# A hybrid decoder step on one core: TensorE leaves mixers' pieces longer in nine projection tiles, the planner's transfer model changes, and the norms' spread product gets 128 rows

## The chip, the core and the metric

The kernel runs on one core of a Trainium2 chip. The metric is the device time of one execution in microseconds; 1324.06 to 1327.06 us were measured for the kernel before, median 1326.87. The engines named here are TensorE (PE in the rows, its weight loader PEld), VectorE (DVE), ScalarE (ACT), GpSimd (POOL) and SyncE (SP), whose queue issues all transfers.

## What is computed

One layer of a hybrid decoder, for a prompt of 1024 rows and 8 sample groups of 8 rows (T = 1088 rows together, width 1024), all in float32:

```python
h = _rmsnorm(x, g_mix_in)
gate_a, x_a, q, k, v, z_c, xbc, dt_raw = _split_cols(h @ w_in)
x_a, lru_buf_new = _causal_conv(x_a, lru_buf, conv_a_w, conv_a_b)
h_a, lru_h_new = _rg_lru(x_a, lru_h0, ...)
out_a = h_a * jax.nn.gelu(gate_a)                          # mixer A
out_b = _combine_branches([... for (w, d) in DILATED])     # mixer B: 6 heads, three dilations
xbc = jax.nn.silu(_causal_conv(xbc, ssd_buf, conv_c_w, conv_c_b)[0])
y_c, ssd_h_new = _ssd(xs, dt, A, Bm, Cm, ssd_h0, chunk)    # mixer C: chunked scan
out_c = _rmsnorm((y_c + d_skip * xs) * jax.nn.silu(z_c), ssm_norm)
x = x + _rmsnorm(concat(out_a, out_b, out_c) @ w_out, g_mix_out)
g_f, u_f = jnp.split(_rmsnorm(x, g_ffn_in) @ w_gate_up, 2, axis=-1)
x = x + _rmsnorm((jax.nn.silu(g_f) * u_f) @ w_down, g_ffn_out)
```

The updated states and the new rows of the key and value caches are outputs too.

## The kernel before

**Layout and products.** Activations lie transposed, 128 features on the partitions and the T rows along them, cut into three groups of 364, 362 and 362 columns (`GROUPS`). Each float32 operand of a large product is split into two rounded parts (float32r), and `mm3` makes one product of three: high with high, high with low, low with high. `x3` makes these three for one block of 128 of the contraction; eight such steps fill a bank for one projection tile and one group.

**Stages.** `w_in` has 23 tiles of 128 outputs. Tiles 0 and 1 are made in `first_products` while the input's norm is taken, tiles 2 to 22 in `projections`, in the order: 2 to 8 the convolved inputs of mixer C, 9 to 11 value, query and key of the first pair of heads, 12 to 14 z, 15 to 17 the second pair of heads, 18 to 20 the third, 21 and 22 the gate. A finished bank goes through `spill` to SBUF or to DRAM (`pd`). Beside this main task run the mixers: `lru`, `convs` and `time_steps`, then `scan` with a `chunk` for each 128 rows, then `attention` (a pair p of heads starts when tile V_T[p] + 2, that is tile 11, 17 or 20, is emitted), `norm_c` and `gate`; their outputs go to `mixd` in DRAM and come back as operands of `w_out`. Then follow `first_out` (first group), `second_half` (waits for `mixers_done`), `gate_up` and `down`.

**The planner.** All instructions are ordered while the program is built. `Flow` keeps a time `now` for TensorE and models of the other engines' queues; `note` takes an operation of VectorE, ScalarE, GpSimd or SP, and `step` emits the one that is ready and has the best rank at the moment when its engine would be idle. A transfer costs QUEUE on SP, then FLIGHT, then its bytes by RATE, one transfer after the other, and its data count as there RECEIPT later. TensorE's own work is in tasks (generators), each of which yields a condition; `run` goes through the tasks in order and advances the first one whose condition holds, mixers ahead of main, so that main's steps fill what the mixers leave. Most of the mixers' conditions ask `ok(...)`: have the operands' writers ended by `now`, with SIGNAL + MARGIN (0.35 us) to spare? The planner's times decide only the order; on the chip every instruction waits for its semaphores, each engine in the order planned.

**The norms.** `inverse_norm` turns a row of sums of squares (128 x w, w about 363) into 1/rms, spread over 128 partitions: three products of one column sum over the partitions, VectorE and GpSimd take the power and split it into two parts, `tr` transposes 128 x 6 values to 6 rows, VectorE spreads these over w columns (6 rows, each non-zero in its own third), and one product with a stationary operand of ones, 6 rows by 128 columns, puts the value of each column on all 128 partitions. The buffer for the 6 rows is the one item of the lane `spread`, 128 x 364 in float32r, of which only rows 0 to 5 are ever written. `inverse_norm` is called by `first_scale` (three times), `norm_c` (three), `out_norm` (twice for each of three groups) and `finish` (two).

Of the kernel before, what the change touches and what calls it, by code (L numbers as in the profile page):

```python
# [35 lines left out]
XA_T, XBC_T, Z_T, GATE_T = 0, 2, 12, 21  # L36
V_T = (9, 15, 18)
W_OUT_T, W_GU_T, W_DN_T = 23, 31, 75
QT = T // 4

PLAIN = 4
PRODUCTS = (1, 6, 2, 7, 5, 4, 3)

# [51 lines left out]
class Rot:  # L95
    def __init__(self, items):
        self.items, self.i = items, -1
# [35 lines left out]
class Flow:  # L133
# [4 lines left out]

    RANKS = {"prep": 0, "norm": 1, "mix": 2, "main": 3}

    SIGNAL, MARGIN = 0.15, 0.2
    QUEUE, FLIGHT, RECEIPT, RATE = 0.475, 0.65, 0.95, 360e3

    def __init__(self):
        self.now, self.tasks = 0.0, []
        self.rank, self.count = 0, 0
        self.idle = {e: 0.0 for e in ("vector", "scalar", "gpsimd", "sync")}
        self.ready = {e: [] for e in self.idle}
        self.dma, self.table = 0.0, None
        self.open = []  # L150
        self.locks = [0.0, 0.0]
        self.place, self.top = {}, 0
        self.wr, self.rd = np.zeros(1 << 18), np.zeros(1 << 18)
# [56 lines left out]
    def ok(self, *aps, write=False):  # L210
        uses = self.uses(aps, write)
        self.advance(self.now)
        return self.done(uses) + self.SIGNAL + self.MARGIN <= self.now and not self.pending(uses)

    def free(self, x):

# [97 lines left out]
    def run(self):  # L314
        idle = 0
        while self.tasks:
            for task in self.tasks:
                if task.cond is None or task.cond():
                    with self.prio(task.cls):
                        try:  # L320
                            task.cond = next(task.gen)
                        except StopIteration:
                            self.tasks.remove(task)
                    idle = 0
                    break
            else:
                self.now += 0.05
                idle += 1
                assert idle < 20000
        self.advance(1e9)  # L330
# [34 lines left out]
class Trunk:  # L365
# [150 lines left out]
    def projections(self):  # L516

        F = self.flow
        for i in range(2, W_OUT_T):
            parts = self.use(i)  # L520
            for g, (c0, w) in enumerate(GROUPS):
                yield lambda: self.lmain.ok() and F.ok(*parts)
                bank = self.lmain.take()
                for k in range(KT):
                    self.x3(bank[:, :w], parts, k, slice(c0, c0 + w), k == 0, k == KT - 1)
                    if k == KT - 1:
                        yield lambda: self.scaled > g
                        if g == 0 and XBC_T < i < XBC_T + 7:
                            yield lambda: self.conv_raws is not None and self.conv_raws.ok()
                            self.padded[i] = self.conv_raws.take()  # L530
                            self.pad(self.padded[i], self.I["ssd_conv"][i - XBC_T])
                        if i >= GATE_T:
                            yield lambda: self.c_done
                        self.spill(i, g, bank[:, :w])
                        self.lmain.give(bank)
                        self.free_at[g] = i + 1
                        if g == 2:
                            self.emitted = i + 1
                    yield None
            if i == DT_AFTER:  # L540
                yield from self.project_dt()
# [28 lines left out]
    def inverse_norm(self, ssum, n, lane, spread):  # L570

        nc, F = self.nc, self.flow
        w = ssum.shape[-1]
        yield lambda: F.ok(ssum) and lane.ok() and self.rstd.ok()
        bank = lane.take()
        at = [min(c, w - 128) for c in range(0, w, 128)]
        b = len(at)
        for c, o in enumerate(at):  # L580
            self.mm(bank[:, c:c + 1], ssum[:, o:o + 128], self.k(K_ONE, 1), start=True, stop=True)
        held = self.rstd.take()
        r, both = held[:, 0:b], held[:, 4:4 + 2 * b].rearrange("p (c q) -> p c q", q=2)
        hi, lo = both[:, :, 0], both[:, :, 1]
        with self.prio("prep"):
            nc.vector.tensor_scalar(r, bank[:, :b], 1.0 / n, EPS, op0=ALU.mult, op1=ALU.add)
            nc.gpsimd.tensor_tensor(r, r, self.half[:, :b], op=ALU.pow)
            nc.vector.tensor_copy(hi.bitcast(F32R), r)
            nc.vector.tensor_sub(lo, r, hi)
        yield lambda: F.ok(both) and spread.ok()  # L590
        rows = bank[0:2 * b, 128:256]
        self.tr(rows, held[:, 4:4 + 2 * b], self.k(K_ID))
        whole = spread.take()
        lent, spread, full = spread, whole[0:2 * b, :w], (b - 1) * 128
        with self.prio("prep"):
            nc.vector.tensor_mul(spread[:, :full].rearrange("p (c t) -> p c t", c=b - 1),
                                 rows[:, None, :].to_broadcast([2 * b, b - 1, 128]),
                                 bc(self.k(K_ROW, b - 1)[0:2 * b], 128))
            nc.vector.tensor_scalar(spread[:, full:], rows[:, 128 - (w - full):], self.k(K_ROW + b - 1, 1)[0:2 * b],
                                    None, op0=ALU.mult)  # L600
        self.rstd.give(held)
        yield lambda: F.ok(spread)
        self.mm(bank[:, :w], self.ones[0:2 * b], spread, start=True, stop=True)
        lent.give(whole)
        return bank

# [58 lines left out]
    def setup(self):  # L665
        nc, I = self.nc, self.I
        xr = [self.alloc(T) for _ in range(8)]
        squares = [self.alloc(364) for _ in range(6)]
        sq, ssum = Rot(squares), self.alloc(T)
        self.splits.append(self.pair())  # L670
        with self.prio("prep"):
            nc.vector.memset(self.half, -0.5)
            self.zeros = self.alloc(256)
            nc.vector.memset(self.zeros, 0.0)
            self.warm(2 * WARM)
            nc.scalar.activation(squares[1][:, 0:4], self.half, AF.Square)
            nc.sync.dma_start(self.cols, I["cols"])
            for k in range(KT):
                g = self.col(C_GMI + k)
                for c0, w in GROUPS if k < 4 else [(0, T)]:  # L680
                    sl = slice(c0, c0 + w)
                    nc.sync.dma_start(xr[k][:, sl], I["xT"][k][:, sl])
                    if k == 0 and c0 == 0:
                        self.first_weights(0, 256)
                    nc.scalar.activation(self.XH[:, k, sl], xr[k][:, sl], AF.Copy, scale=g)
                    nc.vector.scalar_tensor_tensor(self.XL[:, k, sl], xr[k][:, sl], g, self.XH[:, k, sl].bitcast(F32),
                                                   op0=ALU.mult, op1=ALU.subtract)
                if k == 1:
                    self.first_weights(256, 1024)
                if k == 4:  # L690
                    self.prep(2)
            nc.sync.dma_start(self.const, I["consts"][:, 0:K_TRI])
            nc.vector.tensor_copy(self.ones, self.k(K_ONE))
            for i in range(2):
                self.pad(self.padded[XA_T + i], I["lru_conv"][i])
            self.pad(self.padded[XBC_T], I["ssd_conv"][0])
            for c0, w in GROUPS:
                sl = slice(c0, c0 + w)
                for k in range(KT):
                    s, x = sq()[:, :w] if k else ssum[:, sl], xr[k][:, sl]  # L700
                    nc.scalar.activation(s, x, AF.Square)
                    if k:
                        nc.vector.tensor_add(ssum[:, sl], ssum[:, sl], s)
        return ssum
# [828 lines left out]
    def make_stream(self):  # L1533


        self.units = [(j, which, (0, 1)) for j in range(PLAIN // 2, NF // 2) for which in range(2)]
        self.units += [(j, which, (1,)) for j in range(PLAIN // 2) for which in range(2)]
        self.items = [lambda pair: self.plain(pair, LATE_T)]
        self.items += [lambda pair, t=W_OUT_T + n: self.plain(pair, t) for n in range(KT - 1)]
        self.plain_base = len(self.items)  # L1540
        for f in range(PLAIN):
            for which in range(2):
# [12 lines left out]
        order = [LATE_T] + [W_OUT_T + n for n in range(KT - 1)]  # L1555
        order += [W_GU_T + which * NF + f for f in range(PLAIN) for which in range(2)]
        self.tiles_of = dict(enumerate(order))
# [526 lines left out]
```

## Time and profile before

| what | value |
|---|---|
| median of three runs (lowest, highest) | 1326.87 us (1324.06, 1327.06) |
| the profiled execution's own time | 1324.27 us |
| its span, first to last instruction | 1322.5 us |
| TensorE busy | 1294.4 us (98%), 8883 matmuls |
| VectorE, ScalarE, GpSimd busy | 931.3 (70%), 557.1 (42%), 46.5 us (4%) |
| mean granted clock of TensorE | 0.996 |

In the rows, `PE bank L434` is a matmul of the helper `mm` (line 434) and `PE bank L438` a transpose; operations of the other engines all carry line 347, where the planner's wrapper records them, so a row is told apart by its tile names and shape. A shape such as `6*128 6x362` on TensorE is rows x columns of the array in use, then the operand that streams. Busy time of TensorE is modelled from pipelined records: full does not mean at its peak, and the loader's pauses say more.

### The profile page before, as it was taken

To read this page: it belongs to the slowest core of one execution; us is meant where nothing else is said; L and a number is where in the kernel's file an instruction comes from. 1 tells how busy PE (TensorE), PEld (TensorE's weight loads), DVE (VectorE), ACT (ScalarE), POOL (GpSimd) and SP (SyncE) were. 2 spreads that over 40 slices of the span, in tenths; PEclk is the share of its full clock that TensorE was granted. 3 is DMA by queue.
4 is the path that set the end of the run, shared out by engine and by line. 5 is a ranking of instruction groups with operands and counts; after the bars stand their busy time and mean duration, and the time that the engine had idled before them with its cause. 6 is when DMAs were issued, how large, how long until landed. Compare 5 with 4: busy or idle time off the path is not lost.

```text
span 1322.5 us, 22885 instructions
## 1 busy us (share of the span) xinstructions
PE 1294.4 (98%) x8883; PEld 1236.8 (94%) x8883; DVE 931.3 (70%) x1867; ACT 557.1 (42%) x1063; POOL 46.5 (4%) x60
## 2 busy tenths in 40 slices
PE   9999999999999999999999999999999999999997
PEld 8999888899899889989999999999999999999786
DVE  7799795764867977789756666666658856557852
ACT  7364461671675874445222222222223442433312
POOL 0000000000000002420000000000000000000000
PEclk9999999999999999999999999999999999999999
DMA  6122466536737446442132212221023566866651
GB/s 215 29 69 73 125 193 186 166 97 193 215 95 195 142 136 189 159 148 92 46 98 98 78 39 81 98 98 66 34 98 130 174 225 214 301 215 195 193 180 48
DMA packets 92922, 179.38 MB, mean 136 GB/s; under 512 B 15010, under 2 KB 60814, under 8 KB 92814
## 3 DMA queue, kind: packets, MB, share of 16 engines
q1 hardware_dynamic: 92814, 177.93, 43.0%
q8 instruction: 69, 1.13, 0.4%
q14 instruction: 39, 0.32, 0.1%
HBM read 138.61 MB, written 39.28 MB: 135 GB/s over the span
## 4 chain that ended last, share of the span: by engine, by line
PE 76%; DVE 9%; DMA 9%; ACT 2%; issue 2%; SPq 1%; DVEq 0%; POOLq 0%; POOL 0%; ACTq 0%
PE bank L434 74%; DVE t L347 9%; ACT t L347 2%; DMA t<-pd 2%; DMA t<-in_w_in_t 2%; PE bank L438 2%; DMA t<-mixd 2%; SPq L347 1%; DMA t<-yd 1%; DMA t<-eacd 1%; DMA t<-in_w_gu_t 0%; DMA t<-hidd 0%; DMA t<-in_w_out_t 0%; DMA mixd<-t 0%; DMA pd<-t 0%
## 5 line engine op out<-in xcount | busy, mean ns | idle before, releaser
L434 PE MATMUL bank<-t,t 128*128 128x272 f32 (+7 forms) x8505 | 1265.1, 311 | 15.7 <-DVE t L347 12.5
L434 PEld LDWEIGHTS bank<-t,t 128*128 128x128 f32 (+1 forms) x8505 | 1197.7, 186 | 64.5 <-DVE t L347 21.1
L347 DVE TENSOR_TENSOR t<-t,t 128x512 fp32r<-128x512 f32 (+13 forms) x599 | 440.1, 760 | 102.2 <-ACT t L347 93.5
L347 ACT CAST t<-t 128x512 fp32r<-128x512 f32 (+7 forms) x314 | 220.6, 724 | 437.1 <-PE bank L434 178.4
L347 DVE TENSOR_TENSOR t<-t,bank 128x272 f32<-128x272 f32 (+4 forms) x283 | 126.5, 454 | 123.0 <-PE bank L434 122.4
L347 DVE TENSOR_TENSOR t<-bank,t 128x512 fp32r<-128x512 f32 (+11 forms) x227 | 111.7, 511 | 77.1 <-ACT t L347 42.0
L347 ACT ACTIVATE t<-t,t 128x128 f32<-128x128 f32 (+17 forms) x212 | 132.6, 666 | 29.3 <-DVE t L347 13.9
L347 ACT ACTIVATE t<-t 128x272 f32<-128x272 f32 (+9 forms) x173 | 91.5, 537 | 112.7 <-DVE t L347 98.6
L347 POOL TENSOR_TENSOR t<-t,t 128x362 f32<-128x362 f32 (+3 forms) x41 | 43.6, 1077 | 1106.4 <-DVE t L347 1097.6
L347 DVE CAST t<-t 128x1024 fp32r<-128x1024 f32 (+6 forms) x91 | 45.1, 496 | 46.5 <-PE bank L434 34.5
L347 ACT COPY t<-bank 128x272 f32<-128x272 f32 (+7 forms) x122 | 44.5, 373 | 76.9 <-PE bank L434 63.9
L347 DVE TENSOR_TENSOR t<-t 128x272 f32<-128x272 f32 (+8 forms) x147 | 68.2, 465 | 5.3 <-ACT t L347 2.0
L347 DVE SCALAR_TENSOR_TENSOR t<-t,t,t 128x1112 f32<-128x1112 f32 (+6 forms) x68 | 56.9, 861 | 6.0 <-ACT t L347 5.2
L438 PE MATMUL bank<-t,t 128*128 128x128 f32 (+5 forms) x354 | 54.1, 274 | 4.8 <-DVE t L347 3.0
L438 PEld LDWEIGHTS bank<-t,t 128*128 128x128 f32 (+5 forms) x354 | 39.6, 138 | 13.4 <-DVE t L347 7.6
L347 ACT ACTIVATE t<-bank 128x272 f32<-128x272 f32 (+7 forms) x55 | 23.4, 429 | 61.4 <-PE bank L434 60.1
L347 DVE CUSTOM_DVE_ANT_0 t<-bank,t 128x512 f32<-128x512 f32 (+4 forms) x75 | 39.9, 548 | 5.5 <-PE bank L434 5.2
L347 ACT CAST t<-bank 128x512 fp32r<-128x512 f32 (+2 forms) x72 | 35.2, 514 | 19.3 <-PE bank L438 18.9
L347 DVE SCALAR_TENSOR_TENSOR t<-t,t,bank 128x362 f32<-128x362 f32 (+4 forms) x55 | 27.9, 549 | 4.0 <-PE bank L434 2.9
L347 DVE SCALAR_TENSOR_TENSOR t<-t,t 128x1024 f32<-128x1024 f32 (+4 forms) x26 | 20.3, 805 | 2.7 <-ACT t L347 1.5
L347 ACT ACTIVATE t<-bank,t 128x362 f32<-128x362 f32 (+1 forms) x29 | 15.5, 561 | 11.5 <-PE bank L434 11.5
L347 DVE SCALAR_TENSOR_TENSOR t<-t 128x54 f32<-128x54 f32 (+5 forms) x33 | 14.7, 447 | 3.9 <-DMA t<-yd 3.1
(20 smaller groups left out, 76.4 us busy)
## 6 DMA issues: line engine op xcount, KB each, us to landing
t<-in_w_dn SPq DMA_DIRECT2D x66, 512.0 KB, 3.7
t<-in_w_gu_t SPq DMA_DIRECT2D x52, 512.0 KB, 4.5
hidd<-t SPq DMA_DIRECT2D x44, 272.0 KB, 2.1
t<-in_w_in_t SPq DMA_DIRECT2D x21, 512.0 KB, 4.4
t<-hidd SPq DMA_DIRECT2D x44, 176.0 KB, 3.8
t<-in_w_out_t SPq DMA_DIRECT2D x15, 512.0 KB, 3.9
t<-pd SPq DMA_DIRECT2D x24, 256.0 KB, 4.4
t<-in_xT SPq DMA_DIRECT2D x24, 181.0 KB, 3.6
```

What stands on the lines that cost most here:

```text
L347: self.flow.note(self.name, what, args, kw, lambda: getattr(self.engine, what)(*args, **kw))
L434: self.flow.product(out, [w, x], start, d, lambda: self.nc.tensor.matmul(out, w, x, **how))
L438: self.flow.product(out, [x], True, d, lambda: self.nc.tensor.transpose(out, x, ident))
```

## The change

Three edits, which share no lines:

- In main's loop over tiles, a flag `patient` is set for tiles 9 to 17. While it is set, `ok` asked by a mixer's task wants 0.5 us more since the operands' last writer (0.85 instead of 0.35 us). Nothing else asks differently.
- The transfer model's RECEIPT goes from 0.95 to 1.25 us and its RATE from 360 to 280 KB per us (KB of 1000 bytes).
- The spread product takes all 128 partitions of the buffer and of the ones; at the start two VectorE copies fill the buffer with zeros.

```diff
@@ -38,6 +38,7 @@
 W_OUT_T, W_GU_T, W_DN_T = 23, 31, 75
 QT = T // 4
 
+PATIENT = 18
 PLAIN = 4
 PRODUCTS = (1, 6, 2, 7, 5, 4, 3)
 
@@ -138,11 +139,11 @@
 
     RANKS = {"prep": 0, "norm": 1, "mix": 2, "main": 3}
 
-    SIGNAL, MARGIN = 0.15, 0.2
-    QUEUE, FLIGHT, RECEIPT, RATE = 0.475, 0.65, 0.95, 360e3
+    SIGNAL, MARGIN, PATIENCE = 0.15, 0.2, 0.5
+    QUEUE, FLIGHT, RECEIPT, RATE = 0.475, 0.65, 1.25, 280e3
 
     def __init__(self):
-        self.now, self.tasks = 0.0, []
+        self.now, self.tasks, self.patient, self.patience = 0.0, [], False, 0.0
         self.rank, self.count = 0, 0
         self.idle = {e: 0.0 for e in ("vector", "scalar", "gpsimd", "sync")}
         self.ready = {e: [] for e in self.idle}
@@ -210,7 +211,7 @@
     def ok(self, *aps, write=False):
         uses = self.uses(aps, write)
         self.advance(self.now)
-        return self.done(uses) + self.SIGNAL + self.MARGIN <= self.now and not self.pending(uses)
+        return self.done(uses) + self.SIGNAL + self.MARGIN + self.patience <= self.now and not self.pending(uses)
 
     def free(self, x):
 
@@ -315,6 +316,7 @@
         idle = 0
         while self.tasks:
             for task in self.tasks:
+                self.patience = self.PATIENCE * (self.patient and task.cls == "mix")
                 if task.cond is None or task.cond():
                     with self.prio(task.cls):
                         try:
@@ -517,6 +519,7 @@
 
         F = self.flow
         for i in range(2, W_OUT_T):
+            F.patient = XBC_T + 7 <= i < PATIENT
             parts = self.use(i)
             for g, (c0, w) in enumerate(GROUPS):
                 yield lambda: self.lmain.ok() and F.ok(*parts)
@@ -600,7 +603,7 @@
                                     None, op0=ALU.mult)
         self.rstd.give(held)
         yield lambda: F.ok(spread)
-        self.mm(bank[:, :w], self.ones[0:2 * b], spread, start=True, stop=True)
+        self.mm(bank[:, :w], self.ones, whole[:, :w], start=True, stop=True)
         lent.give(whole)
         return bank
 
@@ -691,6 +694,8 @@
                     self.prep(2)
             nc.sync.dma_start(self.const, I["consts"][:, 0:K_TRI])
             nc.vector.tensor_copy(self.ones, self.k(K_ONE))
+            for o in (0, 364 - 256):
+                nc.vector.tensor_copy(self.spread.items[0][:, o:o + 256], self.zeros)
             for i in range(2):
                 self.pad(self.padded[XA_T + i], I["lru_conv"][i])
             self.pad(self.padded[XBC_T], I["ssd_conv"][0])
```

## Rows read from the trace of the kernel before

**Rows 1.** Windows by stage: busy us (instructions) of each engine, granted clock, DMA.

```profile
139.00:330.00 191.00, 185.71 (x1306) 167.84 (x1305) 132.74 (x334) 88.13 (x196) 3.15 (x6) 1.00 0.56 165
401.00:509.00 108.00, 100.72 (x655) 93.27 (x654) 88.29 (x222) 76.41 (x156) 0.00 (x0) 0.98 0.55 158
509.00:602.00 93.00, 90.64 (x591) 87.53 (x591) 74.47 (x132) 41.55 (x73) 34.89 (x30) 0.98 0.52 164
602.00:1210.00 608.00, 607.71 (x4535) 607.13 (x4535) 401.23 (x703) 192.80 (x349) 0.00 (x0) 1.00 0.38 124
```

**Rows 2.** Timeline of SP: issue of the spills and of mixer outputs.

```profile
142.54 0.33 SPq L347 DMA_DIRECT2D pd<-t  x1
...
300.09 1.50 SPq L347 DMA_DIRECT2D mixd<-t  x2
...
328.87 0.32 SPq L347 DMA_DIRECT2D pd<-t  x1
...
400.15 0.51 SPq L347 DMA_DIRECT2D pd<-t  x1
```

**Rows 3.** Groups by line, TensorE, 139 to 330: busy, mean, idle and releaser.

```profile
L434 PE MATMUL bank<-t,t 128*128 128x362 f32 (+11 forms) x1170 | 176.0, 319 | 5.1 <-DVE t L347 5.1
```

**Rows 4.** Weight loads by shape, whole span: busy us, mean ns, idle before.

```profile
L434 PEld LDWEIGHTS bank<-t,t 128*128 128x128 f32 x8025 | 1164.7, 189 | 47.0 <-DVE t L347 14.6 <-issue 8.0 <-ACT t L347 4.5
...
L434 PEld LDWEIGHTS bank<-t,t 6*128 6x128 f32 x14 | 2.5, 181 | 3.9 <-DVE t L347 1.9 <-issue 1.7
```

**Rows 5.** Timeline of the loader around one spread product.

```profile
541.45 0.18 PEld L434 LDWEIGHTS bank<-t,t 6*128 6x128 f32 x1 [0.23 <-issue]
541.80 0.46 PEld L434 LDWEIGHTS bank<-t,t 128*128 128x128 f32 x3 [0.17 <-issue]
```

**Rows 6.** Windows of TensorE with one spread product and without.

```profile
319.31:320.96 1.65, 1.65 (x10) 1.00 0.40 148
317.60:319.25 1.65, 1.65 (x12) 1.00 0.81 207
```

**Rows 7.** Timeline of TensorE, 139 to 509: start, length, count, pause before.

```profile
157.65 4.73 PE L434 MATMUL bank<-t,t 128*64 128x128 f32 x40 [1.33 <-DVE t L347]
...
239.13 4.04 PE L434 MATMUL bank<-t,t 128*128 128x128 f32 x23 [1.11 <-DVE t L347]
...
314.34 2.92 PE L434 MATMUL bank<-t,t 128*128 128x1 f32 x18 [0.95 <-DVE t L347]
...
333.26 1.09 PE L438 MATMUL bank<-t,t 128*128 128x128 f32 x8 [0.98 <-DMA t<-pd]
...
401.22 11.55 PE L434 MATMUL bank<-t,t 128*128 128x364 f32 x69
...
413.78 0.41 PE L434 MATMUL bank<-t,t 128*128 128x384 f32 x1 [1.01 <-ACT t L347]
...
414.95 9.83 PE L434 MATMUL bank<-t,t 128*128 128x384 f32 x49 [0.75 <-DVE t L347]
...
435.20 6.81 PE L434 MATMUL bank<-t,t 128*128 128x364 f32 x37 [1.02 <-ACT t L347]
...
508.92 6.43 PE L434 MATMUL bank<-t,t 128*128 128x1 f32 x30 [2.13 <-DVE t L347]
```

**Rows 8.** Timeline of VectorE at the start.

```profile
4.43 0.60 DVE L347 SCALAR_TENSOR_TENSOR t<-t,t,t 128x364 fp32r<-128x364 f32 x1 [3.27 <-ACT t L347]
```

**Rows 9.** DMA issues: count, KB of one, median us to landing.

```profile
t<-in_w_dn SPq DMA_DIRECT2D x66, 512.0 KB, 3.7
...
t<-in_w_in_t SPq DMA_DIRECT2D x21, 512.0 KB, 4.4
...
t<-pd SPq DMA_DIRECT2D x24, 256.0 KB, 4.4
```

**Rows 10.** The chain that ended last, in order of time, one piece.

```profile
404.10 7.16 DMA t<-pd
```

**Rows 11.** Window of TensorE: granted clock after the busy columns.

```profile
410.00:420.00 10.00, 8.24 (x39) 7.51 (x38) 7.97 (x19) 5.69 (x10) 0.00 (x0) 0.83 0.69 172
```

## Prediction, made before the changed kernel was run

> **What bounds the kernel now.** I read the stage windows first: TensorE is busy for 607.71 of the 608 us from 602 to 1210, so in the second half only shorter TensorE work can save time; before that it is busy for 185.71 of 191 us, 100.72 of 108 and 90.64 of 93 [rows 1]. The matmul stream is the bound and its pauses are what there is to win: 5.3, 7.3 and 2.4 us in the three stretches. Tiles 9 to 17 run from about 139 to 330 us: their first spill to DRAM is issued at 142.54, the last of tile 17 at 328.87, that of tile 20 at 400.15 [rows 2]. Then come TensorE's pauses with their releasers, VectorE first among them [rows 3]. Busy is modelled, though, so I also read the weight loader beside the matmuls, where a lost slot shows as a pause although the busy column is full, and last the times from DMA issue to landing.
>
> **The spread product with 128 rows.** There are 14 of them [rows 4]: three in the input's norm, three in mixer C's, six in the two norms behind w_out, two in the last. Around each the loader pauses twice, for nothing that the profile names: at 541.45 the six-row weights are loaded after a pause of 0.23 us, at 541.80 the next 128 rows after 0.17 [rows 5]; the same stands at each one that does not wait for VectorE, while between other products of the stream it does not pause. That is 0.40 us, 14 x 0.40 = 5.6 us. The other price: a stretch of 1.65 us with the product has 10 matmuls, the like stretch just before it 12 [rows 6]; a slot of this size is 11.55/69 = 0.167 us [rows 7], so two are 0.33 us and the 14 are 4.7 us. I take 5.1, ends 4.7 and 5.6, and zero if the rival below is right. All 14 stand among products that TensorE has queued behind them, so what they give back shortens the path. The product's columns stay the same, so its own streaming does not change. Added are two VectorE copies of 128x256; the nearest row is a larger operation, 0.60 us for 128x364, so at most 1.2 us together. They need only the zeros, and VectorE idles 3.27 us before 4.43 [rows 8]: that idle hides them. Were they put later, at their place in the code, VectorE would carry them in front of the sums of the first norm; by 1.2 us at the most that norm, and the bank it frees, would come later.
>
> On this part two pages differ. The Trainium skill ("TensorE: Matmul & The Clock Gate", section "Why this matters for your kernels") says that a single product with a contraction of 32 takes the same time as one of 128, which would make this part worth 0; and for the load alone the rows agree, 181 ns with six rows and 189 with 128 [rows 4]. The Trainium skill ("TensorEngine Tiling (Array Packing)", section "Key Properties") says that a change of tiling mode drains TensorE, which would make it worth what the two pauses show; the pauses are there [rows 5], and they agree with this one; the sum rests on the pauses alone.
>
> **Patience in tiles 9 to 17.** While main is in these tiles, a mixer's piece counts its operands as ready half a microsecond later in the planner's time, and the planner puts main's step (three products, 3 x 0.167 = 0.5 us) in front of it. On the chip the piece then meets its operands later by about one such step, and a pause of TensorE in front of it shrinks by up to 0.5. All pauses in this stretch that wait for VectorE add up to 5.1 us [rows 3]: 1.33, 1.11 and 0.95 are shown [rows 7], five smaller ones, none over 0.6, share the other 1.7. Taking 0.5 off the three long ones and 1.6 of the rest gives 3.1 us. Upper end 5.1, lower end 0: the pieces' shape stays, and so do the drains between shapes.
> What is late next? With the pieces move the VectorE and ScalarE operations that read their banks, and on SP their stores (yd, mixd) behind main's spills; nothing of main waits for those stores. GpSimd has only the norms' powers and a few memsets there. What the mixers lose is slack that they have: the next head pair needs tile 17's spill (328.87) and the last one tile 20's (400.15) [rows 2], so from there they wait for main, and main comes earlier by what is saved. From tile 18 on the patience is off, and mixers go first again.
>
> **The transfer model.** For 512 KB the planner expected 0.475 + 0.65 + 1.46 + 0.95 = 3.53 us and will expect 0.475 + 0.65 + 1.87 + 1.25 = 4.25; the rows say 4.4 for w_in and 3.7 for w_dn. For 256 KB of pd it was 2.80 and will be 3.31; the row says 4.4 [rows 9]. So pieces that wait for a transfer are planned 0.5 to 0.7 us later: nearer for the first half, too late by 0.55 for w_dn, where TensorE is full and the prefetch hides it. It costs no instruction; it only changes orders: VectorE's and ScalarE's queues meet fewer transfers under way, and TensorE's pieces stand behind more of main's. Pauses behind transfers, from 330 on, are 0.98, 1.01, 0.75, 1.02 and 2.13 us, in sum 5.9 [rows 7]; the pair at 413.78 stands behind the landing of pd after 7.16 us [rows 10]. Half a microsecond off each of the first four is 2.0 us. Against it, the stage from 401 to 509 ends in a wait of 2.13 us for the mixers' last input [rows 7], so later planned pieces lengthen there what ends the stage: a chain of about six transfers (spill, load, mixd and back, twice around) x 0.6 us = 3.6 us if each were put behind one more step. And every order that is planned anew makes pauses of its own. I take 0, ends -5.9 and +3.6.
>
> **The clock.** The granted clock is 0.83 from 410 to 420 [rows 11], so it sat at 1.2 instead of 2.4 GHz for about a third of that, which costs 10 x 0.17 = 1.7 us; the 0.98 of the stretch from 509 to 602 is about as much, 93 x 0.02 = 1.9 [rows 1]. TensorE had paused twice (1.01 and 0.75) about the first and for 2.13 us before the second [rows 7]. If the pause goes, 1.7 can go with it; a new long pause elsewhere would bring one. I take 0, ends -3.4 and +1.7.
>
> **The sum.** -5.1 - 3.1 + 0 + 0 = -8.2 us. The profiled execution took 1324.27 us (span 1322.5 and 1.8 around it), the median of the three runs shown is 1326.87 (1324.06 to 1327.06). From the one the sum gives 1316.1, from the other 1318.7; I take 1317.5.
>
> **The rivals.**
> *Only the norms pay.* Pauses that patience closes come back at other pieces, because all orders up to 600 us are planned anew. For it: VectorE is the releaser nearly everywhere [rows 3, 7], and its work does not shrink. Against: TensorE has main's work to put in front wherever patience is on. Time: 1325.6 (midway between the two bases) - 5.1 = 1320.5.
> *The 128 rows give nothing*: the pauses belong to the product's switch of weights and bank, not to its row count. For it: the load time does not depend on rows [rows 4]. Against: every product of the stream switches weights, and most without a pause. Then 1325.6 - 3.1 = 1322.5. It is the rule of the Trainium skill ("TensorE: Matmul & The Clock Gate") named above.
> *Slower: the mixers end later.* Between 401 and 509 main has only two projection tiles and the first output products beside the last head pair, and TensorE already pauses 7.3 us [rows 1]. What the second head pair still has open when tile 20 is spilled (400.15) comes on top there. The first pair has 74 waits that patience lengthens (5, 7, 9 and 11 for its units of each head, ten for the new tokens and V); with two units in flight 37 stand in a row, 18 us at one step (0.5 us) each, and between its last stores near 300 and tile 17's last spill lie 29 us [rows 2]. It decides when the delay passes 29 us; at a whole microsecond each it is 37, so 8 us of mixers' work move into the full stage, and the transfers' 3.6 us come on top: 1325.6 + 11.6 - 5.1 = 1332.
> *More than the sum.* Corrected transfers close the pauses at 333, 413 and 435 and the clock's first fall with them: 2.0 to 3.8 and 1.7 more, so 1325.6 - 8.2 - 3.7 (or 5.5) is 1312 to 1314, and with the second fall 1310.
>
> **How the numbers follow.** Forecast 0.55 (1314 to 1320), only the norms 0.18, no gain from the rows 0.07, slower 0.09, more than the sum 0.11. A time below 1322.9 is faster by over 0.3% (what a measurement here can tell from no change), above 1330.9 slower. The forecast, the larger gain, half of the second case and a little of the third make 0.76: faster 0.76, slower 0.05 (half of its case), the same 0.19. The range goes to 1309 below, with both falls of the clock gone, and to 1326.5 above, where only the slower case is left out.
>
> **What would show it.** No weights of 6 rows any more, 14 more of 128, and no pauses of 0.23 and 0.17 us around them: the norms are right. Pauses behind VectorE of about 2 us instead of 5.1 in tiles 9 to 17, and tile 17's last spill before 325: patience is right. If the spill is early but tile 20's is not, or the pauses from 401 to 509 grow past 7.3, the gain was handed back. Shorter pauses at the places of [rows 7] from 330 on would show the transfer model. The prediction is wrong if the pauses stay with 128 rows, or if the mixers' end moves behind 509.

## The result, and the profile after

The changed kernel takes 1309.64 us (median; 1308.27 to 1311.66), the kernel before 1326.96: 17.3 us less. The ratio is 0.9887, with a 95% interval of 0.9868 to 0.9906; by the ratio the gain is 15.0 us. The profiled executions are 1308.27 us after and 1324.27 before, 16.0 us apart. The forecast was 1317.5 in a range of 1309 to 1326.5, so the time lies just inside the range, at its low end: the gain was about twice what the sum gave, and the parts that made it are mostly not those that the sum named.

First the stages, as in [rows 1] (busy us and count for PE, PEld, DVE, ACT, POOL, then clock, DMA share, GB/s):

```profile
139.00:330.00 191.00, 188.93 (x1339) 171.47 (x1338) 136.94 (x346) 89.73 (x200) 3.99 (x7) 1.00 0.59 174
401.00:509.00 108.00, 105.40 (x701) 99.11 (x700) 94.15 (x231) 79.73 (x162) 5.49 (x5) 1.00 0.57 169
509.00:602.00 93.00, 91.76 (x641) 90.87 (x641) 80.49 (x135) 45.11 (x76) 27.93 (x26) 0.98 0.50 157
602.00:1210.00 608.00, 606.71 (x4496) 604.78 (x4495) 384.83 (x683) 208.71 (x370) 0.86 (x1) 1.00 0.37 122
```

TensorE pauses 2.1 instead of 5.3 us in tiles 9 to 17 and 2.6 instead of 7.3 in the stage of the last head pair, which has 701 matmuls in the same 108 us instead of 655. The places of [rows 2]: a mixer's store, the last spills of tiles 17 and 20, and behind them the mixers' last store to `mixd`:

```profile
321.56 0.46 SPq L349 DMA_DIRECT2D mixd<-t  x1
...
324.40 0.32 SPq L349 DMA_DIRECT2D pd<-t  x1
...
389.55 0.38 SPq L349 DMA_DIRECT2D pd<-t  x1
...
484.15 0.45 SPq L349 DMA_DIRECT2D mixd<-t  x1
```

Tile 17 is 4.5 us earlier, tile 20 already 10.6. TensorE's two groups between 139 and 330, as in [rows 3], wait 0.2 and 1.6 us for VectorE instead of 5.1:

```profile
L436 PE MATMUL bank<-t,t 128*128 128x362 f32 (+12 forms) x1194 | 178.0, 318 | 0.2 <-DVE t L349 0.2
L440 PE MATMUL bank<-t,t 128*128 128x128 f32 (+3 forms) x145 | 21.9, 276 | 1.8 <-DVE t L349 1.6
```

Of the pauses of [rows 7] from 330 on, the pair at 413.78 has become one of 0.91 us, that at 435.20 stands at 427.46, and the 2.13 us before the norm behind `w_out` are gone: the mixers end while main still has output products to make. The longest that is left before 602 is at 554.57 (TensorE's timeline: start, length, count, pause before):

```profile
409.45 7.58 PE L436 MATMUL bank<-t,t 128*128 128x384 f32 x44 [0.91 <-DVE t L349]
...
427.46 3.55 PE L436 MATMUL bank<-t,t 128*128 128x128 f32 x18 [0.99 <-DVE t L349]
...
554.57 4.32 PE L436 MATMUL bank<-t,t 128*128 128x1 f32 x24 [1.14 <-DVE t L349]
```

All pauses of TensorE from 139 to 602 us add up to 5.5 us instead of 15.5. One thing that changed ahead of TensorE is seen at ScalarE. Its waits for transfers between 401 and 520 us (us in total, times, longest), before:

```profile
ACT t L347 <- DMA t<-pd: 4.9, 2, 4.2
ACT t L347 <- DMA t<-mixd: 4.7, 4, 1.6
ACT t L347 <- DMA t<-in_w_out_t: 2.8, 2, 2.2
```

and after:

```profile
ACT t L349 <- DMA t<-pd: 2.8, 1, 2.8
ACT t L349 <- DMA t<-in_w_out_t: 0.6, 1, 0.6
ACT t L349 <- DMA t<-mixd: 0.2, 1, 0.2
```

ScalarE stood 12.4 us in front of transfers that had not landed; now 3.6. That this is what closes TensorE's pauses is not shown, and other kernels below speak against it. Weights of six rows are gone [rows 4 to 6]: the loader's group of 128 rows has 14 more and its unexplained pauses ("issue") fall from 8.0 to 4.3 us:

```profile
L436 PEld LDWEIGHTS bank<-t,t 128*128 128x128 f32 x8039 | 1165.8, 189 | 37.3 <-DVE t L349 11.4 <-issue 4.3 <-ACT t L349 1.6
```

The two added copies lie in VectorE's first idle time [rows 8], at 1.20 us, 0.62 us together:

```profile
1.20 0.62 DVE L349 CAST t<-t 128x256 fp32r<-128x256 f32 x2
```

The planner's times decide more than the order. `round`, which makes the high part when an operand is split, asks `lightest` which of VectorE and ScalarE would be done with it first by the planner's times, and gives the work to that one. VectorE's splits of 128x1024 fell from 39 to 14, before and after:

```profile
L347 DVE CAST t<-t 128x1024 fp32r<-128x1024 f32 x39 | 27.0, 693 | 35.2 <-PE bank L434 27.9 <-DMA t<-in_w_dn 5.2 <-DMA t<-in_w_out_t 1.4
L349 DVE CAST t<-t 128x1024 fp32r<-128x1024 f32 x14 | 9.7, 692 | 4.2 <-DMA t<-in_w_in_t 2.0 <-DMA t<-in_w_dn 1.6 <-PE bank L436 0.4
```

Between 139 and 602 us, where the pauses were, it made 13 of them and makes 12: nearly all that moved lies behind 602, where TensorE was full already, so this is not what closed the pauses.

### The profile page after: what moved, and what is told of

Same layout as the page of the kernel before. It is cut to its first block, busy times and chain, and to the rows that moved or that the text cites. A ratio compares the mean times of both kernels' runs of the same rounds, so it can differ in the third digit from the quotient of the medians.

```text
span 1306.5 us, 22834 instructions
## 1 busy us (share of the span) xinstructions
PE 1286.5 (98%) x8883; PEld 1234.5 (94%) x8883; DVE 916.9 (70%) x1844; ACT 581.1 (44%) x1088; POOL 45.2 (3%) x60
## 4 chain that ended last, share of the span: by engine, by line
PE 81%; DVE 8%; DMA 4%; ACT 4%; issue 2%; SPq 1%; DVEq 0%; POOLq 0%; POOL 0%; ACTq 0%
PE bank L436 79%; DVE t L349 8%; ACT t L349 4%; DMA t<-in_w_in_t 2%; PE bank L440 2%; SPq L349 1%; DMA t<-pd 1%; DMA t<-eacd 0%; DMA t<-in_w_out_t 0%; DMA t<-mixd 0%; ACT L349 0%; DVEq L2075 0%; POOLq L2075 0%; POOL t L349 0%; DVEq L349 0%
## 5 line engine op out<-in xcount | busy, mean ns | idle before, releaser
L436 PE MATMUL bank<-t,t 128*128 128x272 f32 (+10 forms) x8505 | 1256.6, 311 | 7.7 <-DVE t L349 6.9
L436 PEld LDWEIGHTS bank<-t,t 128*128 128x128 f32 (+2 forms) x8505 | 1195.3, 185 | 49.5 <-DVE t L349 13.5
L349 ACT CAST t<-t 128x512 fp32r<-128x512 f32 (+7 forms) x339 | 246.4, 749 | 388.0 <-PE bank L436 165.9
L349 DVE TENSOR_TENSOR t<-bank,t 128x362 f32<-128x362 f32 (+13 forms) x227 | 112.2, 511 | 75.1 <-ACT t L349 41.3
L349 ACT COPY t<-bank 128x272 f32<-128x272 f32 (+8 forms) x122 | 44.4, 373 | 100.7 <-PE bank L436 85.7
L349 DVE TENSOR_TENSOR t<-t 128x272 f32<-128x272 f32 (+7 forms) x147 | 67.4, 460 | 3.3 <-ACT t L349 0.3
L349 DVE SCALAR_TENSOR_TENSOR t<-t,t,t 128x1112 f32<-128x1112 f32 (+7 forms) x68 | 56.7, 861 | 4.8 <-ACT t L349 3.8
L349 DVE CAST t<-t 128x512 fp32r<-128x512 f32 (+6 forms) x68 | 27.9, 413 | 15.5 <-PE bank L436 6.9
L349 ACT ACTIVATE t<-bank,t 128x362 f32<-128x362 f32 (+1 forms) x29 | 15.5, 559 | 10.3 <-PE bank L436 10.3
```

Of the source, the lines that this page charges most:

```text
L349: self.flow.note(self.name, what, args, kw, lambda: getattr(self.engine, what)(*args, **kw))
L436: self.flow.product(out, [w, x], start, d, lambda: self.nc.tensor.matmul(out, w, x, **how))
```

## The experiments

Each part was run alone and in combinations, then the parts' sizes were varied. Ratios are to the kernel before, run in between: its own median was 1326.96 us beside the whole change, 1322.84 beside n_norms, p_patience, m_model and pm_patience_model, 1323.96 beside pm100, m_receipt, m_rate and m_near, 1323.9 beside the others. So medians of different groups are compared through their ratios. The last two columns are read from the profiled execution of each: when the last store to `mixd` is issued, which is the mixers' end, and the sum of TensorE's pauses from 139 to 602 us.

| kernel | norms | patience | RECEIPT, RATE | median us | ratio (95% interval) | mixers' end | pauses |
|---|---|---|---|---|---|---|---|
| the kernel before | 6 | 0 | 0.95, 360 | 1322.84 to 1326.96 | 1 | 497.52 | 15.5 |
| n_norms | 128 rows | 0 | 0.95, 360 | 1320.37 | 0.9978 (0.9963 to 0.9993) | 494.10 | 15.1 |
| n64_norms64 | 64 rows | 0 | 0.95, 360 | 1326.06, one execution | none | 499.75 | 16.0 |
| p_patience | 6 | 0.5 | 0.95, 360 | 1339.63 | 1.0128 (1.0111 to 1.0145) | 509.67 | 22.3 |
| p100 | 6 | 1.0 | 0.95, 360 | 1322.55 | 0.9981 (0.9963 to 0.9999) | 492.69 | 11.7 |
| m_model | 6 | 0 | 1.25, 280 | 1312.11 | 0.9925 (0.9905 to 0.9945) | 485.88 | 5.3 |
| pm_patience_model | 6 | 0.5 | 1.25, 280 | 1313.36 | 0.9927 (0.9912 to 0.9941) | 486.69 | 8.2 |
| pm100 | 6 | 1.0 | 1.25, 280 | 1312.35 | 0.9911 (0.9892 to 0.9930) | 480.82 | 7.0 |
| nm_norms_model | 128 rows | 0 | 1.25, 280 | 1309.26 | 0.9884 (0.9863 to 0.9904) | 486.32 | 8.5 |
| the whole change | 128 rows | 0.5 | 1.25, 280 | 1309.64 | 0.9887 (0.9868 to 0.9906) | 484.15 | 5.5 |
| m_receipt | 6 | 0 | 1.25, 360 | 1323.75 | 0.9997 (0.9984 to 1.0010) | 495.53 | 12.4 |
| m_rate | 6 | 0 | 0.95, 280 | 1309.77 | 0.9895 (0.9878 to 0.9911) | 478.90 | 7.4 |
| m_near | 6 | 0 | 1.35, 260 | 1316.17 | 0.9943 (0.9928 to 0.9959) | 481.84 | 8.6 |
| nm_over | 128 rows | 0 | 1.6, 220 | 1327.68 | 1.0021 (1.0006 to 1.0036) | 477.11 | 7.5 |

The mixers' end sorts all 14 kernels by the rate. With 360 it lies between 492.69 and 509.67 us and the pauses add up to 11.7 to 22.3; with 280 or less between 477.11 and 486.69, and to 5.3 to 8.6. The two ends that come nearest to each other, of p100 with 360 and of pm_patience_model with 280 (SP's timeline):

```profile
492.69 0.45 SPq L349 DMA_DIRECT2D mixd<-t  x1
...
486.69 0.45 SPq L349 DMA_DIRECT2D mixd<-t  x1
```

### The norms alone

```diff
-        self.mm(bank[:, :w], self.ones[0:2 * b], spread, start=True, stop=True)
+        self.mm(bank[:, :w], self.ones, whole[:, :w], start=True, stop=True)
```

(with the two copies that fill the buffer)

> The spread product with 128 rows alone, orders unchanged. Theory (the pauses belong to the six rows): 14 x 0.38 us, so 4.5 to 5.6 us less than before (1321.5 on a median of 1326.9), the loader's pauses around the 14 products gone, and both falls of the clock where they were. Rival (the pauses belong to the switch of weights and bank): within 1 us of before, pauses of 0.23 and 0.17 us still there.

Measured: 0.9978, some 2.9 us, less than either end of the theory, though the interval (0.9 to 4.9 us) reaches into it. The weights of six rows are gone, and the loader's unexplained pauses at its 128-row weights fall from 8.0 to 4.4 us, so the theory of the rows holds. Why the gain is smaller is not shown. TensorE's timeline of this kernel at three places of [rows 7]:

```profile
329.47 1.09 PE L438 MATMUL bank<-t,t 128*128 128x128 f32 x8 [1.56 <-DMA t<-pd]
...
411.43 0.41 PE L434 MATMUL bank<-t,t 128*128 128x384 f32 x1 [2.07 <-ACT t L347]
...
505.82 4.37 PE L434 MATMUL bank<-t,t 128*128 128x1 f32 x27 [2.38 <-DVE t L347]
```

These pauses were 0.98, 1.01 and 2.13: TensorE comes earlier and waits longer here, 1.9 us together. But other pauses are shorter, and from 139 to 602 they add up to 15.1 us instead of 15.5; and the profiled execution itself took 1317.09 us, 3.3 less than the median. "Both falls of the clock where they were" did not hold in it: the one at 411.43 stands, and behind the 2.38 us at 505.82 the granted clock stays at 1.00:

```profile
505.00:515.00 10.00, 9.18 (x58) 9.11 (x59) 8.33 (x17) 3.83 (x7) 1.95 (x2) 1.00 0.63 223
```

### The product with 64 rows

```diff
+        self.mm(bank[:, :w], self.ones[0:64], whole[0:64, :w], start=True, stop=True)
```

(with the two copies)

> The spread product with 64 rows instead of 128 (58 of them zeros). Theory (the pauses come with every product that does not use all rows of the array): pauses of about 0.23 and 0.17 us around each of the 14 as with six rows. Rival (they come with very few rows): no pauses, as with 128.

Its one execution took 1326.06 us. The loader's timeline around the product of [rows 5]:

```profile
543.59 0.18 PEld L434 LDWEIGHTS bank<-t,t 64*128 64x128 f32 x1 [0.22 <-issue]
543.95 0.46 PEld L434 LDWEIGHTS bank<-t,t 128*128 128x128 f32 x3 [0.17 <-issue]
```

The pauses are those of six rows. At 6 and at 64 rows they come with a product that leaves rows of the array out, not with how many, and 128 rows end them.

### Patience alone

```diff
+    SIGNAL, MARGIN, PATIENCE = 0.15, 0.2, 0.5
...
+            F.patient = XBC_T + 7 <= i < PATIENT
```

> Patience in tiles 9 to 17 alone. Theory (slack of the first head pair): 3.1 us less (2 to 5), TensorE's pauses behind VectorE between 139 and 330 us fall from 5.1 to about 2, the stage of the third head pair as before, with its 2.13 us at the end and its fall of the clock. Rival (the parts work only together, or another plan is what helps): within 2 us of before, or slower, with the saved pauses back between 401 and 509.

Measured: 1.0128, 17 us more. In tiles 9 to 17 it does what was expected (187.79 of 191 us busy instead of 185.71), and the loss comes where patience is off. Its stages:

```profile
401.00:509.00 108.00, 96.05 (x616) 86.87 (x614) 86.83 (x225) 74.40 (x159) 2.75 (x3) 0.97 0.50 147
509.00:602.00 93.00, 87.70 (x543) 84.98 (x544) 66.01 (x110) 39.81 (x71) 24.75 (x25) 0.96 0.51 157
602.00:1210.00 608.00, 604.46 (x4528) 603.16 (x4528) 404.21 (x711) 196.28 (x352) 3.19 (x2) 1.00 0.36 122
```

and the longest of TensorE's pauses there:

```profile
430.14 0.88 PE L440 MATMUL bank<-t,t 128*128 128x128 f32 x6 [3.10 <-ACT t L349]
...
498.28 1.40 PE L436 MATMUL bank<-t,t 128*128 128x1 f32 x10 [3.16 <-DVE t L349]
...
536.61 4.97 PE L436 MATMUL bank<-t,t 128*128 128x1 f32 x21 [2.85 <-DVE t L349]
```

TensorE pauses 12.0 us from 401 to 509 instead of 7.3, 5.3 from 509 to 602 instead of 2.4 and 3.5 in the second half instead of 0.3, and the granted clock is lower (0.97 and 0.96). The 3.10 us at 430.14 wait for ScalarE, which stood before transfers for 17.1 us between 401 and 520 (12.4 before).

### Patience of 1.0

> Patience of 1.0 instead of 0.5 us, transfer model and norms of before. Patience of 0.5 alone was 1.3% slower, with its new pauses after tile 17, where patience is off. Theory A (the delay itself pushes the mixers' end out): slower still, 1.02 or more, with the first head pair's stores later again. Theory B (the old transfer model makes plans whose pauses differ by chance, patience only draws another one): no order in the size, between 0.995 and 1.013, pauses at other places between 400 and 620 us.

Measured: 0.9981, not slower. So the loss at 0.5 is no price of the delay (theory A falls), and the mixers' end, 509.67 us at 0.5, is 492.69 at 1.0. What is left is theory B, an order with more pauses that the planner came upon when the times shifted; which moved operation makes it was not isolated.

### The transfer model alone, and with patience

```diff
-    QUEUE, FLIGHT, RECEIPT, RATE = 0.475, 0.65, 0.95, 360e3
+    QUEUE, FLIGHT, RECEIPT, RATE = 0.475, 0.65, 1.25, 280e3
```

> The new transfer model alone. Theory A (the parts add up): what the whole change gave beyond norms and patience, 17.3 - 5.1 - 3.1 = 9 us less, most of it between 401 and 509, where pauses behind transfers were 4.9 us and the clock fell. Theory B (as in the prediction): within 3 us of before, gains at the pauses behind transfers paid back by the later end of the mixers. Theory C (any new plan draws new pauses): anything from 5 us less to 5 us more, with pauses at other places.

> Patience and transfer model without the norms' part; its plan is that of the whole change but for two copies at the start. If the norms' part adds without regard to the plan: 17.3 - 5 = 12 us less than before. If the parts add, this is the sum of the two single ones. If it is clearly more than their sum, they work together.

Measured: 0.9925 and 0.9927. The model alone gives 10 us (theory A, 9 us), and patience adds nothing to it: alone it lost 17 us, here 0.3. The parts do not add, and not in the way that one helps the other: patience is worth nothing measurable with the new model and brought a bad order with the old one. Both are a further 0.4% above the whole change, near the 5.3 us that 14 pairs of pauses were to give.

Where the model alone gains is seen in its stages, as in [rows 1]:

```profile
139.00:330.00 191.00, 190.45 (x1349) 173.19 (x1348) 137.66 (x345) 93.33 (x204) 3.99 (x7) 1.00 0.58 174
401.00:509.00 108.00, 104.01 (x682) 97.69 (x681) 94.70 (x231) 80.12 (x165) 7.66 (x6) 0.98 0.55 167
509.00:602.00 93.00, 91.87 (x622) 89.15 (x622) 75.19 (x130) 43.59 (x73) 25.04 (x24) 0.98 0.47 149
```

TensorE pauses 0.6, 4.0 and 1.1 us there instead of 5.3, 7.3 and 2.4: 9.3 us less, nearly all of the 10. Half of it lies in tiles 9 to 17, whose pauses the prediction had left to patience. "Most of it between 401 and 509" was wrong, then. ScalarE's waits for transfers from 401 to 520 are 8.9 us in this kernel, not far below the 12.4 of before, so they are not what most of its gain comes from.

### The whole change without patience

> The whole change without patience. Theory (with the new transfer model patience is worth nothing, since the model alone gave -0.75% and model with patience -0.73%): the same as the whole change, a ratio near 0.989. The norms' part then gives its full 14 x 0.38 = 5.3 us on top of the model's, 0.9925 - 0.004 = 0.9885. Rival (the three parts need each other, or the norms give only the 0.22% that they gave alone): 0.9905 or above.

Measured: 0.9884, the whole change's 0.9887 within a tenth of the interval. With the model, the norms' part comes out at its full price: 0.9925 - 0.9884 = 0.0041, 5.4 us. Each of the two ratios is uncertain by 0.002, so the difference is uncertain by some 4 us and cannot be told from the 2.9 us that the norms gave alone. The pauses behind VectorE in tiles 9 to 17 are as short without patience as with it (0.2 and 0.3 us):

```profile
L434 PE MATMUL bank<-t,t 128*128 128x362 f32 (+12 forms) x1206 | 179.8, 318 | 0.2 <-DVE t L347 0.2
L438 PE MATMUL bank<-t,t 128*128 128x128 f32 (+3 forms) x146 | 21.6, 275 | 0.5 <-DVE t L347 0.3
```

### Patience of 1.0 with the new model

> New transfer model and patience of 1.0 us, norms of before. With the old model patience of 0, 0.5 and 1.0 gave 1, 1.013 and 0.998: no order. Theory (the new model makes the plans alike whatever the patience): 0.9925 within 0.003, as with 0 and 0.5. Rival (the model too only drew a good plan): as far apart as with the old one, so outside 0.989 to 0.996.

Measured: 0.9911. With the new model patience of 0, 0.5 and 1.0 gives 0.9925, 0.9927 and 0.9911; with the old one 1, 1.0128 and 0.9981. The first three lie within 0.0016 of each other, as the theory had it, the others 0.0147 apart.

### Which half of the model

> RECEIPT 1.25 alone, RATE stays 360. A transfer of 512 KB then counts as there after 3.83 us, one of 256 KB after 3.10 (before 3.53 and 2.80, with both 4.25 and 3.31). Theory (nearer to the measured landing is better, step by step): about half of the model's gain, 0.995 to 0.998. Rival (chance of the plan): anywhere from 0.99 to 1.01.

> RATE 280 alone, RECEIPT stays 0.95: 3.95 us for 512 KB, 3.01 for 256 KB, and more between transfers that follow one another. Theory (step by step): about half of the model's gain, 0.994 to 0.998. Rival (chance of the plan): anywhere from 0.99 to 1.01.

Measured: 0.9997 and 0.9895. The receipt alone gives nothing in the end, the rate alone all of it and perhaps more (the intervals of 0.9895 and 0.9925 overlap). "Step by step" is wrong, then: the halves are not alike. The receipt is not without effect, though: it takes TensorE's pauses up to 602 from 15.5 to 12.4 us, and pays the 3 us back in the second half, in two pauses that the kernel before did not have (TensorE's timeline):

```profile
621.92 4.80 PE L434 MATMUL bank<-t,t 128*128 128x272 f32 x36 [0.68 <-DVE t L347]
629.83 82.39 PE L434 MATMUL bank<-t,t 128*128 128x272 f32 x639 [3.11 <-DVE t L347]
```

ScalarE's waits for transfers from 401 to 520, with the receipt:

```profile
ACT t L347 <- DMA t<-in_w_out_t: 6.0, 3, 4.5
ACT t L347 <- DMA t<-pd: 2.2, 1, 2.2
ACT t L347 <- DMA t<-mixd: 2.2, 1, 2.2
```

with the rate:

```profile
ACT t L347 <- DMA t<-in_w_out_t: 2.1, 3, 0.8
ACT t L347 <- DMA t<-pd: 0.7, 1, 0.7
```

10.4 us against 2.8. These waits do not sort the kernels by time, however: with both halves they are 8.9 us (9.7 with the norms), and nm_over, the slowest of the later models, has 1.3. What follows is an argument from the planner's code, not shown by a run. A receipt is added once to each transfer, whatever stands before it. The planner lays transfers one behind the other, so the rate's error grows along a row of them: one of 512 KB and five of 256 KB are there after 5.1 us at 360 and after 6.6 at 280, without the fixed parts. And 360 is not what the transfers of the mixers' stages move. Windows of the kernel before in which the DMA engines are nearly full, three of these stages and two of others (last two columns: share, GB/s):

```profile
220.00:230.00 10.00, 9.89 (x65) 9.56 (x64) 4.75 (x21) 2.51 (x6) 0.00 (x0) 1.00 0.87 275
330.00:340.00 10.00, 9.02 (x61) 8.57 (x60) 7.15 (x27) 3.53 (x7) 0.85 (x1) 1.00 0.88 273
400.00:410.00 10.00, 9.91 (x62) 9.61 (x61) 6.64 (x29) 3.12 (x8) 0.00 (x0) 1.00 0.92 229
...
10.00:20.00 10.00, 9.07 (x54) 8.45 (x53) 8.26 (x14) 9.71 (x18) 0.00 (x0) 1.00 1.01 368
...
1130.00:1140.00 10.00, 10.00 (x65) 10.00 (x64) 7.38 (x13) 5.72 (x12) 0.00 (x0) 1.00 1.05 391
```

275/0.87, 273/0.88 and 229/0.92 are 316, 310 and 249 KB per us if they were full: 280 lies among them, 360 above all. At the start and in `down`, 368/1.01 and 391/1.05 are 364 and 372, so there 360 is right and 280 too low: no one rate fits all stages.

### Later still

> A transfer model one step later than the new one, RECEIPT 1.35 and RATE 260: 4.49 us for 512 KB. Theory (a broad best near the measured 3.7 to 4.5 us): 0.9925 within 0.003. Rival (chance of the plan): outside that. With RECEIPT 1.6 and RATE 220 a load of weights was planned behind three large transfers and TensorE paused 8.9 us; if that place is back, the pause is near 1135 us and the fall of the clock behind it.

> Norms and a transfer model that is later still: RECEIPT 1.6 and RATE 220 instead of 1.25 and 280, so 512 KB count as there after 5.1 us where 3.7 to 4.5 were measured. Theory A (what helps is that the model is near the truth): slower than norms with the new model by 3 us or more, since pieces stand behind work that could have waited. Theory B (what helps is any delay that keeps TensorE, ScalarE and VectorE off transfers under way): the same or faster. Theory C (each plan draws its own pauses): anywhere within 8 us of it.

Measured: 0.9943 for 1.35 and 260, within 0.003 of 0.9925 as expected, and its second half has no long pause (0.5 us in all); 1.0021 for 1.6 and 220 with the norms, 0.0137 or 18 us above the same kernel with the new model. By the time, theory A came true: near the measured times was best of what was tried. But up to the mixers' end nm_over loses nothing: it comes first of all, at 477.11, and the pauses of 7.5 us are no more than the 8.5 of nm_norms_model. In that stage every later model did as well (theory B). The 18 us are lost behind, and the largest piece has one place, the longest pause in the second half of nm_over:

```profile
1145.79 0.95 PE L434 MATMUL bank<-t,t 128*128 128x352 f32 x2 [8.88 <-ACT t L347]
```

SP's timeline just before it:

```profile
1126.47 5.61 SPq L347 DMA_DIRECT2D t<-x1d  x3
1132.18 3.53 SPq L347 DMA_DIRECT2D t<-in_w_dn  x1
```

Three transfers of 1.4 to 1.5 MB were issued ahead of the weights that TensorE needed next; ScalarE waits 12.3 us for these (`in_w_dn`) and TensorE for ScalarE. How often such orders come up by chance with each pair of constants was not tried.

## Why the prediction came out as it did, step by step

**The bound, and where there was something to win: right.** Matmuls end the time; the gain lies in the pauses up to 602 us and in the 14 products. The second half did not move (606.71 of 608 us). Between the profiled executions, 10.0 us of pauses, the 5.1 of the norms and the 1.7 of the clock make 16.8, near the 16.0 measured.

**The norms: right in size, as far as the runs can tell.** 5.1 us (4.7 to 5.6) was forecast, 5.4 came with the new model and 5.3 between pm_patience_model and the whole change, both uncertain by 3 to 4 us. Alone it was 2.9 (0.9 to 4.9); whether "what they give back shortens the path" fails in part there, or the measurements only scatter, is open. The rival of no gain falls: with 128 rows the pauses are gone, with 64 they stay. The Trainium skill ("TensorEngine Tiling (Array Packing)", section "Key Properties") has the drain at a change of tiling mode, and both kernels agree with it. The Trainium skill ("TensorE: Matmul & The Clock Gate", section "Why this matters for your kernels") gives a single product with a contraction of 32 the time of one of 128; for a single product inside a stream of 128-row products these runs do not bear that out, since with 6 and with 64 rows the stream loses the 0.22 to 0.23 and 0.17 us beside it. The copies lay where they were put.

**Patience: wrong.** The sum had -3.1 us for it; beside the new model no measurement tells it from nothing (+1.3 and +0.4 us by the medians at 0.5), and alone it cost 17 us. The step that failed is "a pause of TensorE in front of it shrinks": that happened in its own stretch with the old model (2.0 us behind VectorE instead of 5.1), but I took the order after tile 18 as given. All later orders are planned from the shifted times. And with the new model those pauses are gone without patience (0.5 us). My test for it was bad as well: pauses of "about 2 us instead of 5.1" came true (1.8), and so they do without patience.

**The transfer model: the mis-sized term.** I took 0 (-5.9 to +3.6); it gave 10 us. I compared single transfers, 0.5 to 0.7 us later each, set four pauses against a longer chain of the mixers and let them cancel. Three things were wrong. Pieces that are planned later did not lengthen the mixers' stage: it ended at 484.15 instead of 497.52, and earlier than before in every kernel with a rate of 280 or less. I counted only pauses from 330 on, but half of what the model alone gave lies in tiles 9 to 17. And I counted the receipt and the rate alike, where the rate alone gave the whole gain. Which of the orders that moved closes which pause stays open.

**The clock: half.** Both falls that the prediction named went with their pauses (0.98 to 1.00 from 401 to 509, and none behind 509), and one new one came at a pause of 1.14 us at 554.57, which is the 0.98 from 509 to 602. Taken as 0, the clock gave back about 1.7 us.

**The rivals.** "Only the norms pay" and "slower" did not happen; "more than the sum", given 0.11, is what did, in part by the mechanism it named: transfers that are planned later close the pauses from 330 on, and those in tiles 9 to 17 besides, which it did not name. Its 1310 is nearer than my 1317.5. For "slower", the condition was half met: the last of the stores between the spills that [rows 2] shows at 300.09 now stands at 321.56, some 20 us later, which is less than the 29 from which it was to decide, and nothing was lost by it. The slowdown that patience alone did bring is an end of the mixers that comes later, by 12 us (509.67); but the delay that I had priced is not its cause, since twice the delay ends them at 492.69.

That the sum of 8.2 came out on the right side is owed to the norms and to a term that I had set to zero. That the time still lies in the range is luck: its lower end stood for both falls of the clock gone, not for a transfer model worth 10 us, and the 3.1 us put down to patience hide a part of the miss.

## What to carry to other kernels

Where an order is planned from modelled times, an optimistic transfer rate can cost more than one late transfer does: here it cost 10 us, and one rule tuned on top of it another 17. Compare the rate with what the profile's windows move when the DMA engines are full, stage by stage, before any waiting rule is tuned, and judge a rule like patience only with the model corrected, since its local pauses tell nothing of the later stages. A model that is late can win in one stage and lose in the next, as 220 did. A small product that uses part of the array's rows inside a full stream can be padded with zeros; see whether the pauses that go come back elsewhere. Norms with the rate of 280 alone would be the next to try (0.9895 - 0.0041, an estimate of 0.985); it was not run.

## What the runs showed of the hardware

Products with 6 and with 64 rows cost the same pauses, 0.22 to 0.23 and 0.17 us at the loader, in a stream of 128 rows. The changed kernel still has 46 weight loads of 64 rows, with 2.5 us of pauses that the profile does not explain in front of them; whether padding would end these was not tried. And in one execution the granted clock fell at a pause of 1.14 us; the window of the changed kernel around it:

```profile
550.00:560.00 10.00, 8.76 (x51) 8.06 (x51) 8.17 (x19) 4.52 (x6) 0.86 (x1) 0.83 0.20 59
```

The granted clock is 0.83 of its full 2.4 GHz there, so a third of the window ran at 1.2. Before, two pauses of that length stood in this stage (TensorE's timeline of the kernel before):

```profile
570.00 3.20 PE L434 MATMUL bank<-t,t 128*128 128x1 f32 x24 [1.13 <-DVE t L347]
574.43 0.27 PE L438 MATMUL bank<-t,t 128*6 128x128 f32 x1 [1.23 <-DVE t L347]
```

There it stayed at 1.00 behind them. The one fall of that stage came after the 2.13 us at 508.92 [rows 7], and in n_norms none came after the 2.38 us at 505.82. So the length of the last pause alone does not decide in these executions; what does was not tried.
